# A two-layer decoder trunk: other PSUM tiles for the attention outputs, one copy that joins all turned halves, an earlier 4-byte copy, and 2 MB loads six blocks later

## The chip, the cores and the metric

The kernel runs on one core of one Trainium2 chip. The metric is the device time of one execution in microseconds. The kernel before takes 1239.11 us, the median of three runs (1236.39 to 1240.38).

The engines are named as the profile names them: PE is TensorE's matmul and PEld its weight load, DVE is VectorE, ACT is ScalarE, POOL is GpSimd, SP is SyncE, which here only issues DMAs.

## The reference, cut to what matters

A residual stream x of 256 tokens and 2048 channels, all float32, goes through two layers. Each ends with `x <- LayerNorm(alpha * x + mixer(x))`.

- Layer 1 is a Mamba-2 mixer: an input projection of 2048 to 10304 columns, a causal convolution of four taps, one chunk of 256 tokens with 64 heads of width 64 and state 128, a gate, a grouped norm, and an output projection of 4096 to 2048.
- Layer 2 is sparse attention. A projection gives the query latent (512), the key-value latent (256), an index key, index weights and a gate of 4096 columns. An indexer scores all keys for each query and keeps the 64 best. 32 heads of width 128 attend to the kept keys, each output is gated, and an output projection of 4096 to 2048 follows.

Per head h of layer 2, with P the probabilities over the kept keys:

```
logits = (q_h . k_h) / sqrt(128), masked to the kept keys
P      = softmax(logits)
o_h    = P v_h
out    = concat_h(o_h * silu(gate_h)) @ w_out
```

## The kernel before, in words

**Weights come as a stream.** All weight matrices are cut into 404 units of up to 512 KB. A unit is loaded on SP's queue into one of four raw buffers (`load`, L99), and split for TensorE into two parts of less precision each: ScalarE writes the upper part `hi` (`convert`, L121), VectorE the rest `lo` (`finish`, L145). There are four buffers of each, and a raw buffer is filled again, with the unit four further on, as soon as its `lo` is written. TensorE uses a unit in three products (upper by upper, upper by rest, rest by upper): this is one *block* of the program. `Stream.run` makes the order of all engines: for block i it first writes the conversions up to unit i + 3, then TensorE's products of unit i, and then lets every *side work* that is active take one step. A side work is a Python generator; each `yield` is the end of its step. `st.side(i, ...)` starts one behind block i. Each engine runs its instructions in exactly this order; between engines the tile framework puts semaphores where data or a buffer is shared. It also keeps engines that read one PSUM tile in the order in which the program names them.

**The heads of layer 2** are units too: for each pair of heads one unit with the weights for keys and values (`pair_a`) and one for queries (`pair_b`), and between the pairs units of the gate projection (`g`, L337). Two pairs and three gates, ten blocks, make up one period with four heads. `evac_steps` copies the pair's keys, values and queries out of PSUM: for keys and queries an upper part on ScalarE (L1006), the rest by a subtraction on VectorE (L1007), and a plain 4-byte copy of the first 128 columns on ScalarE (L1008). `head_steps` is one head in nine steps: the logits `lg` (L1017 to L1020); mask and maximum on VectorE (L1028); the exponential on ScalarE (L1033); division on VectorE (L1038), GpSimd's copy of the probabilities into separate upper and lower 16-bit halves (L1042), and a DMA transpose of the halves on SP's queue (L1044); an empty step; GpSimd's copy `ptf` that joins the turned halves to 4-byte numbers (L1048); ScalarE's upper part (L1055), ScalarE's `p2`, the last 128 columns (L1056), and VectorE's rest (L1058); an empty step; the output `o` on TensorE (L1062 to L1065). The steps behind that multiply by the gate on VectorE (`og`, L1068) and split the product for the output projection (L1075, L1077).

**PSUM** has eight tiles in four pools: `acc` with three, `y` with two, `m` with two, `s` with one. In the heads `acc` takes keys, values and gates, `s` the queries, and `y` both the logits and the outputs in turn. `m` serves the transposes and the indexer before the heads and a partial sum at the very end.

**Behind the heads** comes the output projection of layer 2, 64 blocks from `n_heads` on (L616 to L618). When the program reaches `n_heads`, heads 28 to 31 are still under way. There GpSimd's queue issues two DMAs of 2 MB each into `fin` (L1346, L1348): the first layer's result, saved in HBM before, and the gain and bias of the last norm, repeated over all partitions. From `n_heads + 7` on, `x1_steps` loads the first norm's gain and bias in pieces (`gb`, L1249) and applies them to `fin` on VectorE (L1255), 20 steps in all. The residual sums of the output projection need this from `n_heads + 28` on.

Of the kernel before, what the change touches and what calls it, by code (L numbers as in the profile page):

```python
# [9 lines left out]
F32 = mybir.dt.float32  # L10
F32R = mybir.dt.float32r
I32 = mybir.dt.int32
U16 = mybir.dt.uint16
AF = mybir.ActivationFunctionType
# [3 lines left out]
P = 128  # L18
T = 256
# [159 lines left out]
def trunk_kernel(ctx: ExitStack, tc: tile.TileContext, x, xt, w1, wdt, dtp, prm, wo1,  # L179
                 wkv, wcq, wix, wg, wab, wo2, lnr, out):  # L180
    nc = tc.nc
# [12 lines left out]
    st = Stream(nc, wraw, whi, wlo)  # L194
# [5 lines left out]
    def y_tile(name):  # L200
        return p_y.tile([P, 512], F32, tag="y", name=name)

    def m_tile(name):
        return p_m.tile([P, 512], F32, tag="m", name=name)
# [780 lines left out]
    def evac_steps(p, names):  # L985
        for nm in names:
            ps = PR[p]["p" + nm]
            if nm == "v":

                hi, lo = (d2.tile([P, T], F32R, tag=f"hv{k}", name=f"hv{p}_{k}", bufs=3)  # L990
                          for k in range(2))
                t = d2.tile([P, T], F32, tag="hv2", name=f"hv{p}_2", bufs=3)
                nc.scalar.activation(hi, ps[:, 0:T], AF.Copy)
                nc.scalar.activation(t, ps[:, T:2 * T], AF.Copy)
                v.tensor_sub(lo, ps[:, 0:T], hi.bitcast(F32))
                PR[p]["v"] = hi, lo, t
                continue


            pp = ps.rearrange("p (k t) -> p k t", k=2)  # L1000
            w = T if nm == "k" else P
            if nm == "q" and p == 0:
                d2.tile([P, 16], F32, tag="gap2", name="gap2", bufs=1)
            hi, lo = (d2.tile([P, 2, w], F32R, tag=f"h{nm}{k}", name=f"h{nm}{p}_{k}") for k in range(2))
            t = d2.tile([P, 2, P], F32, tag=f"h{nm}2", name=f"h{nm}{p}_2")
            nc.scalar.activation(hi, pp[:, :, T - w:T], AF.Copy)  # L1006
            v.tensor_sub(lo, pp[:, :, T - w:T], hi.bitcast(F32))  # L1007
            nc.scalar.activation(t, pp[:, :, 0:P], AF.Copy)  # L1008
            PR[p][nm] = hi, lo, t
        yield  # L1010

    def head_steps(h):
        p, k = divmod(h, 2)
        (qh, ql, q1), (kh, kl, k1) = ([a[:, k, :] for a in PR[p][nm]] for nm in "qk")
        vh, vl, v2 = (a[:, k * P:(k + 1) * P] for a in PR[p]["v"])
        pl = y_tile(f"lg{h}")
        nc.tensor.matmul(pl[:, 128:384], qh, kh, start=True, stop=False)  # L1017
        nc.tensor.matmul(pl[:, 128:384], qh, kl, start=False, stop=False)
        nc.tensor.matmul(pl[:, 128:384], ql, kh, start=False, stop=True)
        nc.tensor.matmul(pl[:, 0:128], q1, k1, start=True, stop=True)  # L1020
        yield
        lg = d2.tile([P, 384], F32, tag="lg", name=f"lgs{h}")
        mx = d2.tile([P, 2], F32, tag="mx", name=f"mx{h}")
        sm = d2.tile([P, 2], F32, tag="sm", name=f"sm{h}")
        rn = d2.tile([P, 2], F32, tag="rn", name=f"rn{h}")
        parts = ((0, 0, 128), (1, 128, 384))
        for j, a, b in parts:
            v.tensor_tensor_reduce(out=lg[:, a:b], in0=pl[:, a:b], in1=mb[:, a:b],  # L1028
                                   scale=-ATT_SCALE, scalar=3.0e38, op0=ALU.add, op1=ALU.min,
                                   accum_out=mx[:, j:j + 1])  # L1030
        yield
        for j, a, b in parts:
            nc.scalar.activation(lg[:, a:b], lg[:, a:b], AF.Exp, scale=-1.0,  # L1033
                                 bias=mx[:, j:j + 1], accum_out=sm[:, j:j + 1])
        yield
        v.reciprocal(rn, sm)
        for j, a, b in parts:
            v.tensor_scalar(lg[:, a:b], lg[:, a:b], rn[:, j:j + 1], 0.5,  # L1038
                            op0=ALU.mult, op1=ALU.mult)
        halves = cmask.bitcast(U16)  # L1040
        turned = d2.tile([P, 768], U16, tag="ptu", name=f"ptu{h}", bufs=1)
        nc.gpsimd.tensor_copy(halves.rearrange("p (a t) -> p a t", a=2),  # L1042
                              lg.bitcast(U16).rearrange("p (t a) -> p a t", a=2))
        nc.sync.dma_start_transpose(turned.rearrange("p (k t) -> p k t", k=6), halves)  # L1044
        yield
        yield
        pt = d2.tile([P, T], F32, tag="ptf", name=f"ptf{h}", bufs=1)
        nc.gpsimd.tensor_copy(pt.bitcast(U16).rearrange("p (t a) -> p a t", a=2),  # L1048
                              turned.rearrange("p (a t) -> p a t", a=2)[:, :, 0:T])
        yield  # L1050
        if h == 0:
            d2.tile([P, 48], F32, tag="gap3", name="gap3", bufs=1)
        ph, pl = (d2.tile([P, T], F32R, tag=f"prT{j}", name=f"prT{h}_{j}") for j in range(2))
        p2 = par[:, P * k:P * (k + 1)]
        nc.scalar.activation(ph, pt[:, 0:T], AF.Copy)  # L1055
        nc.scalar.activation(p2.bitcast(U16).rearrange("p (t a) -> p a t", a=2),  # L1056
                             turned.rearrange("p (a t) -> p a t", a=2)[:, :, T:384], AF.Copy)
        v.tensor_sub(pl, pt[:, 0:T], ph.bitcast(F32))  # L1058
        yield
        yield  # L1060
        po = y_tile(f"o{h}")
        nc.tensor.matmul(po[:, 0:T], vh, ph, start=True, stop=False)  # L1062
        nc.tensor.matmul(po[:, 0:T], vh, pl, start=False, stop=False)
        nc.tensor.matmul(po[:, 0:T], vl, ph, start=False, stop=False)
        nc.tensor.matmul(po[:, P:T], v2, p2, start=False, stop=True)  # L1065
        yield
        og = d2.tile([P, T], F32, tag="og", name=f"og{h}", bufs=1)
        v.tensor_mul(og, po[:, 0:T], GT.pop(h))  # L1068
        if h == 0:
            OG.append(big.tile([P, KT, 2 * T], F32R, tag="A", name="og0"))  # L1070
        if h == 16:
            OG.append(big.tile([P, KT, 2 * T], F32R, tag="C", name="og1"))
        dst = OG[h // 16][:, h % 16, :]
        yield
        nc.scalar.activation(dst[:, 0:T], og, AF.Copy)  # L1075
        yield
        v.tensor_sub(dst[:, T:2 * T], og, dst[:, 0:T].bitcast(F32))  # L1077
        yield
# [3 lines left out]
    for p in range(NH2 // 2):  # L1082
        src = wab[2 * p]
        i = st.add(wab[2 * p], 1024, pair_a(p), KEYS)
        st.side(i, (evac_steps, p, ("k", "v")))
        i = st.add(wab[2 * p + 1], 1024, pair_b(p), STILL)
        st.side(i, (evac_steps, p, ("q",)))
        if p == 0:
            st.extra[i + 1] = 64
        st.side(i + 3, (head_steps, 2 * p))  # L1090
        st.side(i + 5, (head_steps, 2 * p + 1))
        n = (left * (p + 1)) // 16 - (left * p) // 16
        for _ in range(n):
            add_gate(next(gates))
    n_heads = len(st.units)
# [106 lines left out]
    o = [0]  # L1202
# [38 lines left out]
    d2 = L["d2"] = heads.enter_context(tc.tile_pool(name="d2", bufs=2))  # L1241
# [98 lines left out]
        normed2b()  # L1340
    L["tail2"] = last

    st.run(n_heads)
    fin = big.tile([P, 4, D], F32, tag="B", name="fin")
    L["r"], gbf = fin[:, 0:2, :], fin[:, 2:4, :]
    nc.gpsimd.dma_start(fin[:, 0:2, :], x1_d)  # L1346
    st.side(n_heads + 7, (x1_steps,))
    nc.gpsimd.dma_start(gbf, lnr[2:4, :].rearrange("(o h) t -> o h t", o=1).broadcast_to([P, 2, D]))  # L1348
    st.run(n_heads + 40)
    heads.close()  # L1350
# [1 line left out]
    for i in range(len(st.units) - 4, len(st.units)):  # L1352
        st.homes[i] = wmore, 0
    wturn = ctx.enter_context(tc.tile_pool(name="wturn", bufs=1))
    turned = [[cqT[:, n, :], (cqT[:, 3, :], ckvT[:, 0, :], ckvT[:, 1, :])[n]]
              for n in range(3)] + [wturn.tile([P, P], F32R, tag="idr", name="idr")]
# [95 lines left out]
```

## Time and profile before

| What | Before |
|---|---|
| median of 3 runs | 1239.11 us (1236.39 to 1240.38) |
| profiled execution, its own time | 1239.31 us |
| its span, first to last instruction | 1237.6 us |
| busy: matmul, weight load | 1212.9 us, 1127.6 us |
| busy: VectorE, ScalarE, GpSimd | 919.4 us, 675.6 us, 132.3 us |
| mean granted clock | 0.996 |

The stages on the time axis: layer 1's input side up to about 490 us, its output projection up to about 660 us, layer 2's projections and indexer up to about 780 us, the heads up to about 1045 us with their last outputs until 1077 us, and layer 2's output projection beside them from 1042 us to the end. In rows of waits the columns are: who waited, for what, us in total, times, the longest. In rows of the timeline: start, length, engine, line, operation, what is written and read, and in brackets the idle time before it and what ended it. A wait is put down to the instruction nearest the semaphore's last step, so its neighbour on the same engine may be the one that counted.

### The profile page before, as it was taken

To read this page: it belongs to the slowest core of one execution; us is meant where nothing else is said; L and a number is where in the kernel's file an instruction comes from. 1 tells how busy PE (TensorE), PEld (TensorE's weight loads), DVE (VectorE), ACT (ScalarE), POOL (GpSimd) and SP (SyncE) were. 2 spreads that over 40 slices of the span, in tenths; PEclk is the share of its full clock that TensorE was granted. 3 is DMA by queue.
4 is the path that set the end of the run, shared out by engine and by line. 5 is a ranking of instruction groups with operands and counts; after the bars stand their busy time and mean duration, and the time that the engine had idled before them with its cause. 6 is when DMAs were issued, how large, how long until landed. Compare 5 with 4: busy or idle time off the path is not lost.

```text
span 1237.6 us, 22921 instructions
## 1 busy us (share of the span) xinstructions
PE 1212.9 (98%) x8887; PEld 1127.6 (91%) x8887; DVE 919.4 (74%) x1651; ACT 675.6 (55%) x1178; POOL 132.3 (11%) x173
## 2 busy tenths in 40 slices
PE   9999999999999999999999999999999999899998
PEld 8999999999999999888888999999999998788886
DVE  6978788887898789666458768777777777467467
ACT  6555555665665556444347555666666665443341
POOL 0001011111110110100000000122222212200000
PEclk9999999999999999999999999999999999899999
DMA  8766666566656665576556655665666556975662
GB/s 295 221 200 193 192 201 199 170 222 203 190 185 214 190 203 176 191 266 200 188 193 209 213 175 165 187 173 162 175 177 179 165 169 211 290 231 188 202 190 101
DMA packets 91229, 243.07 MB, mean 196 GB/s; under 512 B 33624, under 2 KB 33760, under 8 KB 90736
## 3 DMA queue, kind: packets, MB, share of 16 engines
q1 hardware_dynamic: 86208, 221.59, 56.6%
q0 software_dynamic: 4912, 20.02, 5.3%
q8 instruction: 70, 1.15, 0.4%
q14 instruction: 39, 0.32, 0.1%
HBM read 231.00 MB, written 4.28 MB: 190 GB/s over the span
## 4 chain that ended last, share of the span: by engine, by line
PE 87%; DVE 6%; ACT 4%; DMA 2%; issue 1%; SPq 0%; POOL 0%; DVEq 0%; ACTq 0%; POOLq 0%
PE acc L337 35%; PE g L337 9%; PE o L616 9%; PE o L617 9%; PE o L618 9%; DVE lo L145 2%; PE y L495 2%; ACT hi L121 2%; DMA ptu<-cmask 1%; PE q L979 1%; PE q L981 1%; PE q L980 1%; DVE lgs L1028 1%; DMA scr<-in_xt_dram 1%; ACT lgs L1033 1%
## 5 line engine op out<-in xcount | busy, mean ns | idle before, releaser
L145 DVE TENSOR_TENSOR lo<-raw,hi 128x1024 fp32r<-128x1024 f32 (+1 forms) x400 | 494.4, 1238 | 250.4 <-ACT hi L121 250.1
L121 ACT ACTIVATE hi<-raw 128x1024 fp32r<-128x1024 f32 (+1 forms) x400 | 417.7, 1050 | 199.7 <-PE o L618 153.1
L337 PE MATMUL acc<-xT,hi 128*128 128x256 f32 (+1 forms) x2496 | 301.4, 277 | 0.0
L337 PEld LDWEIGHTS acc<-xT,hi 128*128 128x128 f32 x2496 | 291.3, 188 | 2.5 <-ACT E L448 1.2
L337 PE MATMUL acc<-xT,lo 128*128 128x256 f32 (+1 forms) x1248 | 156.7, 277 | 0.0
L337 PEld LDWEIGHTS acc<-xT,lo 128*128 128x128 f32 x1248 | 148.3, 188 | 0.1
L337 PE MATMUL g<-x1T,hi 128*128 128x256 f32 (+1 forms) x1024 | 125.6, 277 | 0.0
L337 PEld LDWEIGHTS g<-x1T,hi 128*128 128x128 f32 x1024 | 120.9, 189 | 0.2
L616 PE MATMUL o<-hi,yg 128*128 128x512 f32 x256 | 100.3, 392 | 0.0
L616 PE MATMUL o<-hi,og 128*128 128x512 f32 (+1 forms) x256 | 100.1, 391 | 0.0
L618 PE MATMUL o<-hi,yg 128*128 128x512 f32 x256 | 99.7, 389 | 0.0
L617 PE MATMUL o<-lo,yg 128*128 128x512 f32 x256 | 99.6, 389 | 0.0
L618 PE MATMUL o<-hi,og 128*128 128x512 f32 (+1 forms) x256 | 99.5, 389 | 0.0
L617 PE MATMUL o<-lo,og 128*128 128x512 f32 (+1 forms) x256 | 99.5, 389 | 0.0
L337 PE MATMUL g<-x1T,lo 128*128 128x256 f32 x512 | 71.1, 284 | 0.0
L397 DVE SCALAR_TENSOR_TENSOR ca<-acc,par,ca 128x255 f32<-128x255 f32 x138 | 66.1, 479 | 3.3
L337 PEld LDWEIGHTS g<-x1T,lo 128*128 128x128 f32 x512 | 63.7, 190 | 0.2
L404 ACT ACTIVATE xs<-ca 128x256 f32<-128x256 f32 x32 | 13.4, 419 | 82.9 <-DVE ca L397 49.5
L618 PEld LDWEIGHTS o<-hi,og 128*128 128x128 f32 x256 | 48.5, 189 | 10.1
L617 PEld LDWEIGHTS o<-lo,og 128*128 128x128 f32 x256 | 48.5, 189 | 9.8
L616 PEld LDWEIGHTS o<-hi,og 128*128 128x128 f32 x256 | 48.6, 190 | 9.6
L616 PEld LDWEIGHTS o<-hi,yg 128*128 128x128 f32 x256 | 48.1, 188 | 10.2 <-ACT hi L121 0.2
(296 smaller groups left out, 1793.2 us busy)
## 6 DMA issues: line engine op xcount, KB each, us to landing
raw<-in_w_dram SPq DMA_DIRECT2D x160, 512.0 KB, 4.0
raw<-in_wo_dram SPq DMA_DIRECT2D x128, 512.0 KB, 4.1
raw<-in_wg_dram SPq DMA_DIRECT2D x64, 512.0 KB, 3.6
raw<-in_wab_dram SPq DMA_DIRECT2D x32, 512.0 KB, 4.0
abc<-acs_d POOLq DMA_DIRECT2D x32, 256.0 KB, 4.7
raw<-in_wcq_dram SPq DMA_DIRECT2D x8, 512.0 KB, 4.6
raw<-in_wkv_dram SPq DMA_DIRECT2D x8, 336.0 KB, 3.1
scr<-in_xt_dram SPq DMA_DIRECT2D x4, 512.0 KB, 6.8
```

What stands on the lines that cost most here:

```text
L121: self.nc.scalar.activation(h, r, AF.Copy)
L145: eng.tensor_sub(*self.halfway.pop(i))
L337: nc.tensor.matmul(ps[:, 0:n], wt, xs[:, kt, c * T:c * T + n], start=(kt == 0 and not lo and c == 0), stop=last and c == (1 - lo), skip_gr ...
L397: v.scalar_tensor_tensor(acc[:, d:], ps[:, :T - d], w(k), acc[:, d:], op0=ALU.mult, op1=ALU.add)
L404: nc.scalar.activation(dst, acc, AF.Tanh)
L495: nc.tensor.matmul(py[ks, c * T + s * P:(c + 1) * T], xsT[:, s, c, ks], ms[c][k][:, ws], start=(c == 0 and s == 0), stop=(s == 1), skip_gr ...
L616: nc.tensor.matmul(ps, ah, hs, start=(kk == 2 * first), stop=False)
L617: nc.tensor.matmul(ps, ah, ls, start=False, stop=False)
L618: nc.tensor.matmul(ps, al, hs, start=False, stop=(kk == 31))
L979: nc.tensor.matmul(ps, h[:, o:o + P], cqT[:, kt, 0:T], start=(kt == 0), stop=False)
L980: nc.tensor.matmul(ps, h[:, o:o + P], cqT[:, kt, T:2 * T], start=False, stop=False)
L981: nc.tensor.matmul(ps, l[:, o:o + P], cqT[:, kt, 0:T], start=False, stop=(kt == 3))
```

## The change

Four edits. First, in `evac_steps` the 4-byte copy of the first 128 columns stands ahead of VectorE's subtraction instead of behind it. Second, `ptf` holds all 384 columns: GpSimd joins all halves in one copy of 768 16-bit elements instead of 512, and ScalarE's `p2` reads 128 joined numbers instead of 256 halves. Third, `o` takes an `m` tile instead of a `y` tile. Fourth, the two 2 MB loads are written behind block `n_heads + 5` and not ahead of block `n_heads`, and `x1_steps` starts at `n_heads + 13`.

```diff
@@ evac_steps
             nc.scalar.activation(hi, pp[:, :, T - w:T], AF.Copy)
+            nc.scalar.activation(t, pp[:, :, 0:P], AF.Copy)
             v.tensor_sub(lo, pp[:, :, T - w:T], hi.bitcast(F32))
-            nc.scalar.activation(t, pp[:, :, 0:P], AF.Copy)
@@ head_steps
-        pt = d2.tile([P, T], F32, tag="ptf", name=f"ptf{h}", bufs=1)
+        pt = d2.tile([P, 384], F32, tag="ptf", name=f"ptf{h}", bufs=1)
         nc.gpsimd.tensor_copy(pt.bitcast(U16).rearrange("p (t a) -> p a t", a=2),
-                              turned.rearrange("p (a t) -> p a t", a=2)[:, :, 0:T])
+                              turned.rearrange("p (a t) -> p a t", a=2))
...
         nc.scalar.activation(ph, pt[:, 0:T], AF.Copy)
-        nc.scalar.activation(p2.bitcast(U16).rearrange("p (t a) -> p a t", a=2),
-                             turned.rearrange("p (a t) -> p a t", a=2)[:, :, T:384], AF.Copy)
+        nc.scalar.activation(p2, pt[:, T:384], AF.Copy)
...
-        po = y_tile(f"o{h}")
+        po = m_tile(f"o{h}")
@@ behind the heads
-    st.run(n_heads)
+    st.run(n_heads + 6)
     fin = big.tile([P, 4, D], F32, tag="B", name="fin")
     L["r"], gbf = fin[:, 0:2, :], fin[:, 2:4, :]
     nc.gpsimd.dma_start(fin[:, 0:2, :], x1_d)
-    st.side(n_heads + 7, (x1_steps,))
+    st.side(n_heads + 13, (x1_steps,))
```

How the instruction order moves on the engines that the prediction speaks of. Each row is a line of the program, an operation, what it writes and reads, and in brackets the engines or DMA queues whose semaphores it waits for; numbers in names count buffers, and lines behind the edit are one lower in the changed kernel.

TensorE in the heads, the piece of the difference with one head's output `o` and the logits `lg` of a later head:

```order
-L1062 MATMUL o_10000<-prT_0_9897,hv_0_9451 128x256 [waits DVE_49,Activation_49]
-L1063 MATMUL o_10000<-prT_1_9898,hv_0_9451 128x256
-L1064 MATMUL o_10000<-prT_0_9897,hv_1_9452 128x256
-L1065 MATMUL o_10000<-par,hv_2_9453 128x128 [waits Activation_49]
-L1017 MATMUL lg_10012<-hk_0_9711,hq_0_9768 128x256 [waits DVE_49]
+L1061 MATMUL o_10000<-prT_0_9897,hv_0_9451 128x256 [waits PE_49,Activation_49]
+L1062 MATMUL o_10000<-prT_1_9898,hv_0_9451 128x256
+L1063 MATMUL o_10000<-prT_0_9897,hv_1_9452 128x256
+L1064 MATMUL o_10000<-par,hv_2_9453 128x128 [waits Activation_49]
+L1017 MATMUL lg_10012<-hk_0_9711,hq_0_9768 128x256
```

The order is the same; the first products of `o` and of `lg` no longer name VectorE among what they wait for.

ScalarE at a pair's evacuation, the piece with keys `hk`, values `hv` and queries `hq`:

```order
 L1006 ACTIVATE hk_0_9711<-k_9671 128x512 [waits PE_49]
-L1008 ACTIVATE hk_2_9713<-k_9671 128x256 [waits DVE_49]
+L1007 ACTIVATE hk_2_9713<-k_9671 128x256
 L993 ACTIVATE hv_0_9717<-v_9672 128x256 [waits PE_49]
 L994 ACTIVATE hv_2_9719<-v_9672 128x256
 L121 ACTIVATE hi_9723<-raw_9542 128x1024 [waits DMAHW2_49,Activation_49]
 L1006 ACTIVATE hq_0_9768<-q_9729 128x256 [waits PE_49]
-L1008 ACTIVATE hq_2_9770<-q_9729 128x256 [waits DVE_49]
+L1007 ACTIVATE hq_2_9770<-q_9729 128x256
 L121 ACTIVATE hi_9774<-raw_9585 128x1024 [waits DMAHW4_49,Activation_49]
```

Nothing moves on ScalarE; the 4-byte copies lose their wait for VectorE.

GpSimd at the end of the heads, first before (`cmask` is the copy into halves, `ptf` the join, `fin` the 2 MB loads, `gb_hk` the first norm's pieces):

```order
L1346 DMA fin<-x_d 128x4096 [waits DMASW3_49,PE_49]
L1348 DMA fin<-in_lnr_dram 128x4096
L1048 COPY ptf_13175<-ptu_13108 128x2x256 [waits DMAHW0_49,DVE_49]
L1042 COPY cmask<-lgs_13111 128x768 [waits DVE_49,Pool_49]
L1048 COPY ptf_13239<-ptu_13180 128x2x256 [waits DMAHW3_49,DVE_49]
L1042 COPY cmask<-lgs_13183 128x768 [waits DVE_49,Pool_49]
L1048 COPY ptf_13297<-ptu_13244 128x2x256 [waits DMAHW6_49,DVE_49]
L1249 DMA gb_hk_13349<-in_lnr_dram 128x512 [waits DMASW6_49]
```

and in the changed kernel:

```order
L1048 COPY ptf_13172<-ptu_13108 128x2x384 [waits DMAHW0_49,DVE_49,Activation_49]
L1042 COPY cmask<-lgs_13111 128x768 [waits DVE_49,Pool_49]
L1048 COPY ptf_13236<-ptu_13177 128x2x384 [waits DMAHW3_49,DVE_49,Activation_49]
L1042 COPY cmask<-lgs_13180 128x768 [waits DVE_49,Pool_49]
L1048 COPY ptf_13294<-ptu_13241 128x2x384 [waits DMAHW6_49,DVE_49,Activation_49]
L1345 DMA fin<-x_d 128x4096 [waits DMASW3_49,PE_49]
L1347 DMA fin<-in_lnr_dram 128x4096
L1248 DMA gb_hk_13470<-in_lnr_dram 128x512 [waits DMASW6_49]
```

The two loads stand behind the last three joins instead of ahead of them, and each join carries 384 columns and also waits for ScalarE, which reads its buffer.

## The prediction

> **What bounds the kernel now.** I read the page first: the span, TensorE's busy share, then the stretches, then who TensorE waits for, then single rows of one such wait. The profiled execution took 1239.31 us with a span of 1237.6, so 1.7 us lie outside the span; the median of the runs shown is 0.2 us lower. I work on the profiled execution and take 0.2 off at the end.
>
> ```profile
> span 1237.6 us, 22921 instructions
> PE 1212.9 (98%) x8887; PEld 1127.6 (91%) x8887; DVE 919.4 (74%) x1651; ACT 675.6 (55%) x1178; POOL 132.3 (11%) x173
> 50.00:661.00 611.00, 611.00 (x4637) 571.00 (x4636) 472.23 (x775) 336.92 (x531) 57.38 (x77) 1.00 0.62 202
> 820.00:1031.00 211.00, 198.17 (x1681) 195.39 (x1682) 158.25 (x357) 133.30 (x318) 46.24 (x48) 0.99 0.61 173
> 961.33:964.74 3.41, 3.41 (x19) 3.41 (x18) 1.56 (x2) 3.41 (x10) 0.00 (x0) 0.50 0.33 95
> 1060.32:1067.14 6.82, 5.35 (x14) 4.29 (x15) 3.71 (x7) 5.14 (x12) 3.32 (x4) 0.50 0.80 244
> ...
> PE o L1062 <- DVE og L1068: 10.7, 7, 1.9
> PE o L1062 <- ACT prT L1055: 4.2, 1, 4.2
> PE o L1062 <- DVE rn L1036: 1.9, 6, 0.3
> PE lg L1017 <- DVE mx L1028: 1.8, 6, 0.3
> ```
>
> The stretches (columns: from:to, length, busy us and instructions of TensorE's matmul, its weight load, VectorE, ScalarE, GpSimd, then granted clock) say that TensorE never stops from 50 to 661 us, and stands for 12.8 of 211 us while the heads run. The waits (total, times, longest) name all four stops: the output matmul `o` waits seven times for `og` and six times for what stands as `rn`, the logits `lg` six times for `mx`, and one long wait stands at the end of the heads. Nothing else holds TensorE for more than a pipeline gap, so an edit is worth what it takes from these rows and no more. The granted clock is 0.50 in two stretches, each behind a long wait.
>
> **Part 1: the output accumulator from the other pair of PSUM tiles.** Now `lg` and `o` take turns in the two `y` tiles, so `o` of a head gets the tile that the `o` before it, or a logits, still holds, and must wait until VectorE has read it. Here is a head without the wait and the next with it:
>
> ```profile
> 846.56 0.28 PE L968 MATMUL v<-hi,ckvT 128*128 128x256 f32 x1
> 846.68 0.28 PE L1062 MATMUL o<-prT,hv 128*128 128x256 f32 x1
> 846.79 0.28 PE L1063 MATMUL o<-prT,hv 128*128 128x256 f32 x1
> 847.16 0.37 PE L1017 MATMUL lg<-hk,hq 128*128 128x256 f32 x1
> ...
> 852.36 1.07 PE L337 MATMUL g<-x1T,lo 128*128 128x256 f32 x8
> 855.11 0.36 PE L1062 MATMUL o<-prT,hv 128*128 128x256 f32 x1 [1.68 <-DVE og L1068]
> 855.30 0.28 PE L1063 MATMUL o<-prT,hv 128*128 128x256 f32 x1
> 846.33 0.42 DVE L1068 TENSOR_TENSOR og<-o,sC 128x256 f32<-128x256 f32 x1
> 948.96 0.42 DVE L1058 TENSOR_TENSOR prT<-ptf,prT 128x256 fp32r<-128x256 f32 x1
> 951.49 0.28 PE L1062 MATMUL o<-prT,hv 128*128 128x256 f32 x1
> ```
>
> With two tiles of its own, the `o` at 855.11 needs only the read two heads back, over at 846.75, while TensorE was free at 853.43: 6.7 us to spare. The logits then wait for the logits two heads back, as far away. So the three rows of 10.7, 1.9 and 1.8 us go: **14.4 us**. A stop costs more than its row. Eight matmuls fill 1.07 us, so they start 0.113 apart and the last before the wait starts at 853.15; `o` starts 1.96 us later where 0.12 is normal, and the next 0.19 behind it where 0.11 is normal: 1.92 us lost for a row of 1.68, 0.24 more. Taken for all 19 stops: **4.6 us**. The half clock at 961 follows the longest of these waits (1.9); 3.41 us of work at half speed lose **1.7 us**.
>
> What is late next: `o` also needs the probabilities' rest, written by VectorE at L1058. The tightest head I found has it done at 949.38 and TensorE there at 951.49, 2.1 us to spare. That is the smallest margin behind which the gain can go, and the first rival.
>
> **Part 2: one join of all halves, and 4-byte copies.** GpSimd's copy grows from 512 to 768 elements, ScalarE's copy of the second part loses its 2-byte steps, and the transposes no longer wait for ScalarE.
>
> ```profile
> L1042 POOL COPY cmask<-lgs 128x768 uint16<-128x768 uint16 x32 | 32.6, 1018 | 206.9 <-DVE mx L1028 116.4 <-DVE lgs L1038 90.4
> L1048 POOL COPY ptf<-ptu 128x512 uint16<-128x512 uint16 x32 | 29.2, 912 | 125.7 <-DMA ptu<-cmask 110.9 <-DVE hv L995 6.7 <-DVE lo L145 4.4
> 847.53 1.69 POOL L1042 COPY cmask<-lgs 128x768 uint16<-128x768 uint16 x1 [0.49 <-DVE lgs L1038]
> 848.45 1.04 DVE L1058 TENSOR_TENSOR prT<-ptf,prT 128x256 fp32r<-128x256 f32 x1
> L1056 ACT ACTIVATE par<-ptu 128x256 uint16<-128x256 uint16 x32 | 15.6, 486 | 0.0
> ACT hq L1008 <- DVE hq L1007: 44.6, 16, 3.3
> ACT hk L1008 <- DVE hk L1007: 22.9, 16, 2.1
> L1008 ACT ACTIVATE hq<-q 128x256 f32<-128x256 f32 x16 | 6.2, 385 | 44.6 <-DVE hq L1007 44.6
> ```
>
> The copy of 768 elements at L1042 takes 1.02 us on average and the one of 512 takes 0.91; half as much again would be 1.37. So the join costs 0.1 to 0.46 us a head, GpSimd being idle most of the stage (46 of 211 us); I take 0.3. It lies in front of `L1058`, whose margin is 2.1 us or more: nothing on the path. It also meets VectorE: the `L1058` under the 1.69 us copy took 1.04 us, against 0.42 elsewhere, so up to 32 x 0.46 = 14.7 us of VectorE's time go with it, none of it TensorE's while margins last. The Trainium skill ("SBUF — State Buffer", section "SBUF: two separate sides") speaks against this edit: the port pair that the two engines share is an exclusive lock, held for a whole instruction while the loser fully blocks. The two rows agree with it; by that rule the 0.46 us would stand in front of `L1058` a second time, as blocked VectorE, and rival (a) below would cost 7 x 0.46 = 3.2 us more, 1221.8.
>
> The swap in the evacuation turns a wait round. ScalarE stands 67.5 us (44.6 + 22.9) for VectorE's subtraction before it may copy the last part of the same PSUM tile; now it copies at once, and VectorE waits for a copy of 0.385 us instead, 32 x 0.385 = 12.3 us at most. ScalarE's conversions come up to 3.3 us earlier, so `L1058`, behind them on VectorE, does too. On the path I count nothing for part 2, in either direction; its worth is that it keeps the margin of part 1.
>
> **Part 3: the two 2 MB loads six blocks later.**
>
> ```profile
> fin<-x_d POOLq DMA_DIRECT2D x1, 2048.0 KB, 10.3
> fin<-in_lnr_dram POOLq DMA_DIRECT2D x1, 2048.0 KB, 14.8
> raw<-in_wo_dram SPq DMA_DIRECT2D x2, 512.0 KB, 14.8
> ptu<-cmask SPq DMA_TRANSPOSE x1, 15.3
> ...
> DMA to landing us min/median/max: 2.5/2.6/15.3
> raw<-in_wo_dram SPq DMA_DIRECT2D x3, 512.0 KB, 7.3
> rx<-in_x_dram POOLq DMA_DIRECT2D x2, 1024.0 KB, 11.2
> ACT hi L121 <- PE o L618: 76.5, 48, 2.3
> ```
>
> The first four rows are the DMA issues between 1044 and 1049 us: issued beside the two loads, the transpose took 15.3 us where the median over the heads (next row) is 2.6, and head 29's `o` waited 4.2 us for its probabilities. In the changed order both loads stand behind the last join, so every transpose is done: the wait goes, **4.2 + 0.24 = 4.4 us**, and with it the half clock from 1060.32, in which TensorE worked 5.35 us: **2.7 us**.
>
> The loads now run beside weight loads alone. A weight load is issued when its buffer is free, four blocks ahead; a block of 24 times 0.113 us lasts 2.72, so ScalarE wants it 4 x 2.72 less 2.3 (the two halves of a conversion) = 8.6 us after issue. Conversions in turn wait for TensorE's buffers (last row above), so they are done three blocks ahead, 8.2 less 2.3 = 5.9 us before TensorE. A weight load may thus take 14.5 us before TensorE stands. Beside the two 1 MB loads at 537 us it took 7.3 (TensorE full, first fence); beside these, behind a slow transpose, 14.8. Between 0 and 0.3 us, then, or up to 3 if several loads in a row are late; no transpose stands in their way now, so I take 0. VectorE's work on what is loaded moves with it and lies under the output projection, where VectorE's queue has that 5.9 us of room.
>
> **The sum.** 14.4 + 4.6 + 1.7 + 4.4 + 2.7 = 27.8 us. 1239.3 - 27.8 = 1211.5 for the profiled execution, **1211.3** against the median. A check by another way:
>
> ```profile
> 781.91 0.28 PE L1017 MATMUL lg<-hk,hq 128*128 128x256 f32 x1
> 812.74 0.37 PE L1017 MATMUL lg<-hk,hq 128*128 128x256 f32 x1
> 820.01 0.36 PE L1062 MATMUL o<-prT,hv 128*128 128x256 f32 x1 [1.00 <-DVE og L1068]
> 1030.88 0.36 PE L1062 MATMUL o<-prT,hv 128*128 128x256 f32 x1 [1.67 <-DVE og L1068]
> ```
>
> The first two rows bound the first ten blocks with four logits, when no stop had come: 30.83 us, plus two outputs that were not yet due (846.68 to 847.16 each, 0.48): 31.8. The last two bound six such periods: 35.15 each. That gives 6 x 3.36 = 20.1 us for this stretch where the rows above give 18.3. I keep the lower and put the difference into the range.
>
> **The rivals.** (a) The rest of the probabilities takes over: TensorE comes up to 2.9 us a period earlier, VectorE does not, and the margin of 2.1 turns into a wait of 0.8 + 0.24 us in each of seven periods: 7.3 us back, **1218.6**. For it: GpSimd's longer copy and VectorE's new wait lie right there. Against it: ScalarE, which is in front, loses 67 us of waiting. (b) Weight loads come late behind the moved loads: 3 + 0.24 us and another half-clock stretch of 1.7: **1216.2**. (c) The half clock at 961 is not the wait's doing: of seven waits of 1.0 to 1.9 us only one has it behind it. Then 1.7 us stay, **1213.0**. The Trainium skill ("TensorE: Matmul & The Clock Gate", "What's actually happening") speaks for it: idle means a window of about 3.4 us, longer than that wait. (d) The change does not do what it says, since the reads that `o` waits for are late for the new tiles too; only part 3 is left, 7.1 us: **1232.0**. The 6.7 us speak against it. (e) Slower: VectorE becomes the bound in the heads. It works 158.25 us in 24 heads, 6.6 each, and TensorE without waits needs 31.8 / 4 = 7.95; the new wait and the join add at most 0.39 + 0.46, so 7.45. It decides from 8.8 a head (35.15 / 4) on; at 9.0 it would give 32 x 0.2 = 6.4 us more, **1245.5**. (f) A wait that no row shows fills the gaps: **1239**.
>
> **How the numbers follow.** Forecast 0.67, (a) 0.12, (b) 0.10, (c) 0.05, (d), (e) and (f) 0.02 each. The forecast's own range is 1208 to 1215; with (a) to (c) the range is 1206.5 to 1220. Within 0.3% (3.7 us) of 1239.1 is about what a measurement of this kernel cannot tell from no change: only (f) lies there. Faster 0.96, same 0.02, slower 0.02.
>
> **What would show it.** Right: no row of TensorE waiting for `og`, `rn` or `mx`; six periods of about 31.8 us; ScalarE no longer waiting at the evacuation of `hk` and `hq`, VectorE there instead; every transpose landed in about 2.6 us; granted clock 1.00 between 800 and the end. Wrong: `o` waiting for `prT`, a weight load behind the moved 2 MB with TensorE standing, or a half-clock stretch without a wait before it.

## The result, and the profile after

The changed kernel takes 1211.07 us, the median of four runs (1209.96 to 1211.45). The kernel before, beside it on the same chip, takes 1239.38 us (1236.39 to 1240.38). The ratio is 0.9774 with an interval of [0.9756, 0.9792]. The forecast was 1211.3 us. The profiled execution takes 1210.82 us, 2.0 of them outside the span.

The head of the page, changed kernel:

```profile
span 1208.8 us, 22955 instructions
PE 1202.2 (99%) x8887; PEld 1121.7 (93%) x8887; DVE 923.5 (76%) x1651; ACT 669.5 (55%) x1178; POOL 137.6 (11%) x173
```

TensorE's waits over the whole span (total, times, longest):

```profile
PE zeros L705 <- DVE scr L700: 1.3, 1, 1.3
PE acc_two L347 <- ACT hi L108: 1.0, 2, 0.6
```

Both rows belong to the first 16 us. Behind them TensorE waits for nothing to the end. The stretches, first before and then changed (columns as in the prediction: from:to, length, busy us of TensorE, its weight load, VectorE, ScalarE, GpSimd, then granted clock, DMA share, GB/s):

```profile
820.00:1004.00 184.00, 172.90 (x1463) 170.28 (x1463) 137.10 (x313) 117.16 (x280) 38.05 (x41) 0.99 0.60 172
```

```profile
820.00:1004.00 184.00, 184.00 (x1609) 184.00 (x1608) 153.77 (x341) 122.70 (x303) 48.23 (x47) 1.00 0.70 191
1060.00:1067.00 7.00, 7.00 (x33) 5.79 (x32) 4.19 (x5) 4.15 (x4) 0.00 (x0) 1.00 0.80 297
50.00:661.00 611.00, 611.00 (x4635) 570.88 (x4634) 472.59 (x775) 336.90 (x532) 56.93 (x77) 1.00 0.62 202
```

TensorE stood 11.1 us of these 184 and now stands for none; layer 1 is as it was; between the start and TensorE's last product no stretch has half clock. The two outputs that bound six periods, in the timeline of TensorE, changed kernel:

```profile
818.26 0.28 PE L1061 MATMUL o<-prT,hv 128*128 128x256 f32 x1
1010.70 0.28 PE L1061 MATMUL o<-prT,hv 128*128 128x256 f32 x1
```

They stand 192.44 us apart, 32.07 a period; the same two stood 210.87 apart before. The heads gave 18.4 us in these six periods.

The waits at the evacuation (changed kernel):

```profile
ACT hq L1006 <- PE q L981: 23.0, 16, 2.0
DVE hk L1008 <- ACT hk L1007: 3.1, 6, 0.6
DVE hq L1008 <- ACT hq L1007: 0.6, 1, 0.6
```

ScalarE's 67.5 us of waiting for VectorE are gone. It now waits for TensorE, and VectorE waits 3.7 us for ScalarE.

The moved loads (at the end of a row: KB each, us from issue to landing) and, for the line that issues the transposes, the time to landing:

```profile
fin<-x_d POOLq DMA_DIRECT2D x1, 2048.0 KB, 9.2
fin<-in_lnr_dram POOLq DMA_DIRECT2D x1, 2048.0 KB, 15.6
```

```profile
DMA to landing us min/median/max: 2.5/2.7/5.5
```

ScalarE's wait for weights between 1030 and 1100 us, and from the timelines of VectorE and TensorE one weight unit behind the loads:

```profile
ACT hi L121 <- DMA raw<-in_wo_dram: 7.9, 3, 3.6
```

```profile
1058.44 1.22 DVE L145 TENSOR_TENSOR lo<-raw,hi 128x1024 fp32r<-128x1024 f32 x1 [3.79 <-ACT hi L121]
1062.66 0.39 PE L617 MATMUL o<-lo,og 128*128 128x512 f32 x1
```

No transpose takes longer than 5.5 us (15.3 before; the median is 2.7, where the prediction has about 2.6 for every one). ScalarE did wait for weights beside the moved loads, 7.9 us. The unit at 1058.44 is the tightest: its rest is written at 1059.66, and TensorE reads it at 1062.66, 3.0 us later and without a stop.

### The profile page after: what moved, and what is told of

Read it like the earlier page. It is cut to its first block, busy times and chain, and to the rows that moved or that the text cites. A ratio compares the mean times of both kernels' runs of the same rounds, so it can differ in the third digit from the quotient of the medians.

```text
span 1208.8 us, 22955 instructions
## 1 busy us (share of the span) xinstructions
PE 1202.2 (99%) x8887; PEld 1121.7 (93%) x8887; DVE 923.5 (76%) x1651; ACT 669.5 (55%) x1178; POOL 137.6 (11%) x173
## 4 chain that ended last, share of the span: by engine, by line
PE 98%; DMA 1%; DVE 0%; issue 0%; SPq 0%; ACT 0%; DVEq 0%
PE acc L337 35%; PE g L337 15%; PE o L616 10%; PE o L617 10%; PE o L618 10%; PE y L495 2%; PE q L979 1%; PE q L980 1%; PE q L981 1%; DMA scr<-in_xt_dram 1%; PE v L966 1%; PE k L959 1%; PE v L968 1%; PE k L957 1%; PE k L958 1%; PE v L967 1%
## 5 line engine op out<-in xcount | busy, mean ns | idle before, releaser
L404 ACT ACTIVATE xs<-ca 128x256 f32<-128x256 f32 x32 | 13.4, 419 | 82.9 <-DVE ca L397 49.4
L616 PEld LDWEIGHTS o<-hi,yg 128*128 128x128 f32 x256 | 48.1, 188 | 10.2 <-issue 0.2
L618 PEld LDWEIGHTS o<-hi,yg 128*128 128x128 f32 x256 | 48.1, 188 | 10.1
L618 PEld LDWEIGHTS o<-hi,og 128*128 128x128 f32 x256 | 48.0, 188 | 9.9
L617 PEld LDWEIGHTS o<-lo,yg 128*128 128x128 f32 x256 | 48.1, 188 | 9.7
```

The lines of the kernel that those rows point to most:

```text
L404: nc.scalar.activation(dst, acc, AF.Tanh)
L616: nc.tensor.matmul(ps, ah, hs, start=(kk == 2 * first), stop=False)
L617: nc.tensor.matmul(ps, ah, ls, start=False, stop=False)
L618: nc.tensor.matmul(ps, al, hs, start=False, stop=(kk == 31))
```

## The experiments

The time was as forecast; the question is whether it went for the reasons given. These runs switch the four edits in and out, in us, each the median of its executions (the kernel before, run beside them, took between 1238.5 and 1239.4):

| m tiles | 4-byte copy sooner | join | loads later | time |
|---|---|---|---|---|
| | | | | 1239.4 |
| x | | | | 1237.7 |
| | | | x | 1232.5 |
| | x | x | | 1216.9 |
| x | | | x | 1228.3 |
| x | | x | x | 1228.1 |
| x | x | | x | 1211.0 |
| | x | x | x | 1211.0 |
| | x | | x | 1211.5 |
| x | x | x | x | 1211.1 |

### Part 1 alone: the m tiles

```diff
-        po = y_tile(f"o{h}")
+        po = m_tile(f"o{h}")
```

> Part 1 alone (the outputs in the m tiles, nothing else). My theory: TensorE's rows for og, rn and mx go with their restarts and the half clock behind them, 14.4 + 4.6 + 1.7 = 20.7 us of 1239.4, so 1218.7; the long stop at the heads' end and the half clock behind it stay. Rival (a), the rest of the probabilities takes over because ScalarE has not been relieved: o waits for prT about 1 us in each of seven periods, 1226. Rival (d), the reads are late for the other tiles too: 1239.

Measured: 1237.7 us, ratio 0.9987 [0.9978, 0.9996], so 1.6 us [0.5, 2.7] and not 20.7. TensorE's waits from 700 us on:

```profile
PE g L337 <- DVE gate L804: 9.9, 10, 1.8
PE o L1062 <- ACT prT L1055: 5.4, 1, 5.4
PE g L337 <- DVE sC L804: 1.0, 1, 1.0
PE v L966 <- DVE gate L804: 0.6, 2, 0.3
PE o L616 <- DVE gate L804: 0.3, 1, 0.3
```

and the stretch of the heads, columns as above:

```profile
820.00:1004.00 184.00, 174.25 (x1492) 172.10 (x1491) 137.27 (x309) 118.40 (x283) 37.98 (x41) 1.00 0.60 173
```

The rows for `og`, `rn` and `mx` are gone, as forecast, and the time is not. TensorE now waits for `acc` tiles that hold a gate, which VectorE has not read yet (L804, written to `gate` or `sC`): 11.8 us in place of 14.4. A new wait took the old one's place, on the same engine, VectorE. All theories fell here; rival (a) had the right form with the wrong buffer (`prT`), rival (d) the right size with the wrong reason.

### Part 3 alone: the loads

```diff
-    st.run(n_heads)
+    st.run(n_heads + 6)
...
-    st.side(n_heads + 7, (x1_steps,))
+    st.side(n_heads + 13, (x1_steps,))
```

> Part 3 alone (the two 2 MB loads and x1_steps six blocks later). My theory: the wait of 4.2 us at the heads' end, its restart of 0.24 and 2.7 us of half clock go, 1239.4 - 7.1 = 1232.3, and every transpose lands in under 6 us. Rival: the weight loads take the delay over and TensorE stands for one, about 5 us back, 1237. The og, rn and mx rows stay at about 14 us; if the half clock near 961 us belongs to the long og wait it is there again, if it is not the wait's doing it may be absent or elsewhere.

Measured: 1232.5 us, ratio 0.995 [0.9934, 0.9967], 6.9 us less where 7.1 were forecast. The stop at the end of the heads and the half clock there are gone, the slowest transpose lands in 4.6 us, and behind the start no wait of TensorE for weights is in the trace. The three rows of `og`, `rn` and `mx` stay with 15.1 us, without a half clock behind any of them.

### Part 2 alone, and parts 1 and 3 without it

> Part 2 alone (the join of all halves and the earlier 4-byte copies). My theory as predicted: nothing on the path, 1239.4 within 1 us. Rival: the relief of ScalarE brings VectorE's work forward, og, rn and mx with it, so that part of the 14.4 us of stops goes: at half of them with their restarts 1230. Rival: the longer join slows VectorE beside it, 7 x 0.46 = 3.2 us more, 1242.6.

> Parts 1 and 3 without part 2. If part 2 is what keeps the margin of part 1, as I predicted, o now waits for prT in up to seven periods, up to 7.3 us above the changed kernel: 1213 to 1218.5. Rival: the margin holds without part 2, TensorE waits for nothing and the time is that of the changed kernel, 1211.1 within 0.7 us.

Measured: 1216.9 us for part 2 alone, ratio 0.982 [0.9806, 0.9835]; 1228.3 us without it, ratio 0.9914 [0.99, 0.9929]. Part 2, which the prediction counted at nothing, brings 22.5 us by itself, twice as much as parts 1 and 3 together (11.1). In the run with part 2 alone, TensorE's only wait from 700 us on, at the end of the heads:

```profile
PE o L1061 <- ACT prT L1055: 2.9, 1, 2.9
```

and the stretch of the heads:

```profile
820.00:1004.00 184.00, 184.00 (x1608) 184.00 (x1608) 154.70 (x340) 122.68 (x303) 50.04 (x47) 1.00 0.66 190
```

The outputs still take turns with the logits in the two `y` tiles, and TensorE does not stop once. In the run without part 2 the waits for the gate tile are back (9.5 us in ten stops, 1.9 for `sC`, and three of 0.3).

### Which half of part 2, and are the m tiles needed at all

```diff
 # the 4-byte copy put back (rest as changed)
-            nc.scalar.activation(t, pp[:, :, 0:P], AF.Copy)
             v.tensor_sub(lo, pp[:, :, T - w:T], hi.bitcast(F32))
+            nc.scalar.activation(t, pp[:, :, 0:P], AF.Copy)
 # the join put back to 512 elements, p2 from halves (another run)
-        pt = d2.tile([P, 384], F32, tag="ptf", name=f"ptf{h}", bufs=1)
+        pt = d2.tile([P, T], F32, tag="ptf", name=f"ptf{h}", bufs=1)
...
 # the outputs back in the y tiles (another run)
-        po = m_tile(f"o{h}")
+        po = y_tile(f"o{h}")
```

> The changed kernel with the 4-byte copies put back behind VectorE's subtraction; the join, the m tiles and the moved loads stay. New theory: VectorE and ScalarE, waiting for each other in turn, are what sets the pace of the heads; ScalarE's 67 us of waiting for the subtraction come back, its weight conversions come late, VectorE waits for them, and TensorE waits for a gate tile that VectorE has not released: as in the run without part 2, 1228, VectorE's waits for hi near 33 us between 820 and 1004. Rival: it is the join (fewer ScalarE steps, a turned buffer that comes free sooner) that brought the time, then 1211 to 1213.

> The changed kernel without the join: GpSimd joins 512 elements, ScalarE writes the last 128 columns from halves; the earlier 4-byte copies, the m tiles and the moved loads stay. New theory: the join is worth nothing, 1211.1 within 1 us, TensorE waits for nothing in the heads. Rival: the join brought part of the gain, above 1214.

> The changed kernel with the outputs back in the y tiles, taking turns with the logits. New theory: TensorE's waits for og, rn and mx came from VectorE running late, not from the tiles; with VectorE on time the tiles do not matter: 1211.1 within 1 us. My prediction, read as it stands: without part 1 the 14.4 us of waits and their restarts stay, about 1230. Between them: the y tiles are free just in time and some outputs wait 0.3 us, 1212 to 1214.

> The kernel before with two edits only: the earlier 4-byte copies and the moved loads; outputs in the y tiles, join of 512 elements. New theory: these two are the whole change, 1211.0 within 1 us, and TensorE waits for nothing from 780 us on. Rival: the join or the m tiles are needed by one another's absence (each was left out alone at no cost), then some outputs wait for og again, 1213 or more.

Measured: without the earlier 4-byte copy 1228.1 us, ratio 0.992 [0.9905, 0.9935]; without the join 1211.0, ratio 0.9784 [0.9767, 0.98]; without the m tiles 1211.0, ratio 0.9784 [0.977, 0.9799]; with nothing but the earlier copy and the moved loads 1211.5, ratio 0.9779 [0.9764, 0.9794]. Two lines exchanged in `evac_steps` and the moved loads are the whole gain. The exchange is worth 21.0 us (1232.5 to 1211.5), the join nothing, the m tiles nothing once the exchange is there.

How a wait of ScalarE holds TensorE is seen in both engines' rows of the kernel before. Timeline of ScalarE, then of VectorE, at one pair's evacuation:

```profile
847.75 0.57 ACT L1006 ACTIVATE hk<-k 128x512 fp32r<-128x512 f32 x1
850.46 0.39 ACT L1008 ACTIVATE hk<-k 128x256 f32<-128x256 f32 x1 [2.13 <-DVE hk L1007]
...
852.22 0.40 ACT L1006 ACTIVATE hq<-q 128x256 fp32r<-128x256 f32 x1
855.89 0.39 ACT L1008 ACTIVATE hq<-q 128x256 f32<-128x256 f32 x1 [3.28 <-DVE hq L1007]
856.17 1.05 ACT L121 ACTIVATE hi<-raw 128x1024 fp32r<-128x1024 f32 x1
```

```profile
851.43 0.42 DVE L995 TENSOR_TENSOR hv<-v,hv 128x256 fp32r<-128x256 f32 x1 [1.00 <-ACT hv L994]
...
855.43 0.42 DVE L1007 TENSOR_TENSOR hq<-q,hq 128x256 fp32r<-128x256 f32 x1
857.25 1.23 DVE L145 TENSOR_TENSOR lo<-raw,hi 128x1024 fp32r<-128x1024 f32 x1 [1.40 <-ACT hi L121]
```

ScalarE has the queries' upper part at 852.6 and then stands until VectorE, which has other work in its queue, reaches the subtraction at 855.43. Behind the standing copy on ScalarE is a weight conversion (856.17), and VectorE, done with its own queue, stands 1.40 us for it. Each engine waits for the other in turn. The waits of both between 820 and 1004 us, before:

```profile
DVE lo L145 <- ACT hi L121: 33.7, 34, 1.4
DVE hv L995 <- ACT hv L994: 10.0, 10, 1.0
DVE hk L1007 <- ACT hk L1006: 0.8, 3, 0.4
...
ACT hq L1008 <- DVE hq L1007: 32.9, 11, 3.3
ACT hk L1008 <- DVE hk L1007: 13.8, 10, 2.1
ACT gate L802 <- PE g L337: 9.6, 5, 2.6
...
ACT sC L802 <- PE g L337: 2.0, 1, 2.0
...
```

and in the changed kernel:

```profile
DVE lo L145 <- ACT hi L121: 25.2, 44, 1.2
...
ACT gate L802 <- PE g L337: 35.2, 14, 3.2
ACT hq L1006 <- PE q L981: 14.9, 11, 2.0
ACT sC L802 <- PE g L337: 10.0, 4, 3.1
...
```

Before, VectorE's 137.1 us of work and 44.5 of waiting for ScalarE fill 181.6 of the 184 us, while ScalarE stands 46.7 us for VectorE's subtractions and 11.6 for TensorE. In the run with part 1 alone ScalarE waits for TensorE not once in these 184 us (49.4 us for the subtractions), and TensorE still stands for 9.75. So the two engines hold each other up in a loop that needs no TensorE, and a period of four heads at its pace takes longer than TensorE's own work: 35.15 us in the kernel before against 32.07 in the changed one. `og`, `mx` and the gate are read late because VectorE is late; which PSUM tile TensorE then stands for is only a matter of which is read last. After the exchange ScalarE stands 60.1 us for TensorE and not at all for the subtractions: TensorE sets the pace. That VectorE's work and waits fill the stretch is no sign by itself, for they still do (153.8 and 28.3 us); what changed is for whom ScalarE stands.

### Standing, or PSUM tiles released late?

The order of the two reads also changes when the tiles of keys and queries come free. Here the copy stands behind the subtraction again, but one block later, when it has nothing to wait for:

```diff
-            nc.scalar.activation(t, pp[:, :, 0:P], AF.Copy)
             v.tensor_sub(lo, pp[:, :, T - w:T], hi.bitcast(F32))
             PR[p][nm] = hi, lo, t
+            later = t, pp
         yield
+        nc.scalar.activation(later[0], later[1][:, :, 0:P], AF.Copy)
+        yield
```

(In the step with keys and values only the keys have such a copy.)

> The changed kernel with the 4-byte copies of keys and queries put one block later, behind the subtraction but not waiting for it, since it is long done by then; the PSUM tiles of keys and queries are released a block (2.7 us) later. If ScalarE's standing is what cost the time: no waits of ScalarE for the subtraction, about 1211 to 1213. If it is the time at which the PSUM tiles are released: TensorE waits for the keys' tile, which the gate or the next unit wants, and 1220 or more.

Measured: 1211.7 us, ratio 0.9788 [0.9774, 0.9803]. The last pair's copy of the keys starts 2.6 us behind their upper part here and 2.7 in the kernel before, that of the queries 3.0 and 3.7, so the tiles come free nearly as late as they did. Later release costs nothing; it was the standing.

### How much standing, and how much work, the loop bears

```diff
-            nc.scalar.activation(t, pp[:, :, 0:P], AF.Copy)
+            if nm == "q":      # "k" in the other run
+                nc.scalar.activation(t, pp[:, :, 0:P], AF.Copy)
             v.tensor_sub(lo, pp[:, :, T - w:T], hi.bitcast(F32))
+            if nm != "q":      # "k" in the other run
+                nc.scalar.activation(t, pp[:, :, 0:P], AF.Copy)
```

> The changed kernel with the earlier 4-byte copy for the queries alone; the keys' copy stands behind the subtraction. Theory of a pace that is set by ScalarE and VectorE waiting for each other: before, ScalarE stood 44.6 us for the queries and 22.9 for the keys; if each microsecond of standing costs the same share of the 17 us between this kernel without the swap (1228.1) and with it (1211.1), the queries are worth 11 us and the remaining stand of the keys costs 6: 1217. Rival: the loop has slack, and with the longer stand gone TensorE sets the pace again: 1211 to 1212.

> The changed kernel with the earlier 4-byte copy for the keys alone; the queries' copy stands behind the subtraction. By the same share the stand for the queries costs 11 us: 1222. Rival: the loop has slack for one of the two: 1211 to 1214.

Measured: queries alone 1211.5 us, ratio 0.9777 [0.9763, 0.9792]; keys alone 1212.0, ratio 0.9782 [0.9766, 0.9798]. So the cost is not a share of the standing: with either copy moved the loop is short enough, and TensorE sets the pace. In the run with the keys alone it is short enough by little. ScalarE's waits between 820 and 1004 us, then the stretch:

```profile
ACT hq L1011 <- DVE hq L1009: 31.3, 11, 3.7
ACT og L1077 <- DVE og L1070: 8.5, 10, 1.3
ACT hq L1006 <- PE q L981: 6.6, 8, 1.2
ACT gate L802 <- PE g L337: 5.6, 4, 1.8
...
```

```profile
820.00:1004.00 184.00, 183.70 (x1602) 183.50 (x1602) 152.88 (x336) 123.92 (x305) 51.98 (x46) 1.00 0.66 186
```

ScalarE still stands 31.3 us for the queries (32.9 before), and TensorE loses 0.30 us in these 184. A long row of waits thus does no harm by itself; with the 13.8 us for the keys beside it, the loop was longer than TensorE's work. How long a period of the loop is in this run no row shows: the two engines' rows look much like a loop here too, and only TensorE's 0.30 us say that it sets the pace.

```diff
-            v.tensor_sub(pl, pt[:, 0:T], ph.bitcast(F32))
+            for _ in range(2):
+                v.tensor_sub(pl, pt[:, 0:T], ph.bitcast(F32))
...
+        for _ in range(2):
             v.tensor_mul(og, po[:, 0:T], gt)
```

> The changed kernel with two of VectorE's operations in each head done twice over (the rest of the probabilities and the product with the gate), 0.66 to 0.84 us more of VectorE a head, 6.7 to about 7.4 us where TensorE needs 8.0. By busy time alone (the reading of my rival e) VectorE still has room: 1211 to 1213. If VectorE's waits for ScalarE's conversions (28 us of 184, 1.2 a head) count as used time too, 7.4 + 1.2 = 8.6 us a head and VectorE sets the pace: 24 heads or more by 0.6, 1225 or above. Between: part of those waits shrinks as VectorE runs later.

Measured: 1211.7 us, ratio 0.978 [0.9765, 0.9795]. The heads, and VectorE's waits there:

```profile
820.00:1004.00 184.00, 184.00 (x1608) 184.00 (x1607) 171.63 (x388) 123.94 (x305) 49.13 (x47) 1.00 0.68 190
```

```profile
DVE lo L145 <- ACT hi L121: 7.8, 17, 0.8
```

VectorE at 171.63 of 184 us, 93%, does not hold TensorE: the added work comes out of its waits (25.2 down to 7.8 us), which are slack as long as ScalarE itself only waits for TensorE. Before, at 75%, VectorE held TensorE. Its busy share tells neither.

## Why the prediction was right, and where its reasons were not

**The sum** was right to 0.2 us because it was taken from TensorE's own stops: whoever removes them all gains that much. Its attribution was wrong in two steps that balance, and that they balance is luck: part 2, at nothing in the sum, was in the bundle, and parts 1 and 3, to which the sum gives everything, bring 11.1 us of the 27.8 without it. The signs of being right came, a median transpose of 2.7 us and a period of 32.07 for 31.8 among them, but they name what TensorE does and not which edit does it: the run with the exchange and the moved loads alone shows no wait of TensorE either.

**Part 1, "So the three rows of 10.7, 1.9 and 1.8 us go".** The rows go by the m tiles (part 1 alone), the time does not: 1.6 us by themselves, 4.2 beside the moved loads (1232.5 to 1228.3), nothing once ScalarE no longer stands. The step that failed is the one behind it, "What is late next". It looked at one successor, the probabilities' rest with 2.1 us to spare, and took the smallest margin found there for the smallest there is; the gate tiles had less. The engine that all those rows name was late as a whole, and a tile more for one reader does not make it sooner.

**Part 2, "On the path I count nothing for part 2".** This is the other failed step: the exchange brings 21.0 us. The row for it was quoted, 67.5 us of ScalarE's standing, and the text even says that conversions come 3.3 us earlier. What was not asked is whether VectorE waits for these conversions, which would have closed the loop. That "its worth is that it keeps the margin of part 1" is right in the letter, for without it the m tiles bring 4.2 us, but part 1 has no worth to be kept.

**The join** was priced rightly at nothing. GpSimd's rows:

```profile
L1048 POOL COPY ptf<-ptu 128x768 uint16<-128x768 uint16 x32 | 41.2, 1286 | 105.1 <-DMA ptu<-cmask 77.6 <-DVE lo L145 11.1 <-DVE lgs L1038 8.2
```

1.286 us against 0.912 before, 0.37 a head where 0.1 to 0.46 was allowed. VectorE's bill is 2.8 us in 184 us of the heads (153.77 busy against the 150.94 of the next row), far under the 14.7 allowed for all of them. The heads in the run without the join:

```profile
820.00:1004.00 184.00, 184.00 (x1608) 184.00 (x1607) 150.94 (x340) 125.75 (x303) 43.69 (x47) 1.00 0.66 190
```

**The restart cost.** Six periods gave 18.4 us; the rows with 0.24 us for each of their 16 stops and the 1.7 us of half clock made 18.3, the cross-check by unstalled periods 20.1. The rows were the better measure: a period takes 32.07 us and not 31.8.

**The 1.7 us of half clock at 961.** They are gone in the changed kernel, and they were gone too in the traced execution of the run with the loads alone, where all the waits were still there. So they need a wait, but do not follow every such wait (last section). Rival (c) is wrong in that nothing of them stays in the changed kernel, and right in that the wait's length alone does not bring them.

**Part 3** was right in size and in mechanism: 6.9 us for 7.1, no slow transpose, and weight loads that come late for ScalarE but not for TensorE (3.0 of 5.9 us of margin left). Rival (b) needs 3 us more delay than was there.

**The other rivals.** (a) did not come: no `o` waits for `prT` in the changed kernel. (e), VectorE as the bound from 8.8 us of work a head on, was weighed by busy time; VectorE was already the bound before, together with ScalarE, at the 6.6 us a head that the prediction gives, and is not at 7.5 in the last run (171.63 in 23 heads).

## What to carry to other kernels

Rows of waits on the engine that sets the end give the size of a gain and not its cause: before an edit is credited, follow the engine that releases late one step back and ask what it waits for itself. Two engines with long rows of waits for each other in the same stretch, while the engine that should set the pace stands, are to be suspected of a loop, and its bound is not seen in any busy share; look for the instruction in one queue that stands for the other with work behind it. Such a loop costs only what it is longer than the next bound, so half of a fix may bring all of the gain, and a row of 31 us of waits may cost next to nothing in one kernel and be part of a loop that costs 21 us in another.

## What the runs showed of the hardware

The half-clock stretches begin on a grid: 961.33 and 1060.32 in the kernel before are 98.99 us apart, 29 times 3.413, and while TensorE has work they last 3.41 or 6.82. Laid over that grid, TensorE's stops sort by how much of one grid window they fill. Two windows, first of the kernel before, then of the run with the loads alone:

```profile
957.92:961.33 3.41, 1.52 (x14) 1.35 (x13) 2.93 (x8) 0.42 (x3) 0.26 (x1) 1.00 0.55 172
```

```profile
920.97:924.38 3.41, 1.75 (x15) 1.58 (x15) 2.80 (x6) 0.74 (x2) 1.80 (x1) 1.00 0.65 178
```

The first, idle for 1.89 of 3.41 us (55%), is followed by half clock; the second, idle for 1.66 (49%), is not. In the traces of the kernel before and of the five runs with parts 1, 2, 3 alone, with parts 1 and 3, and with the 4-byte copy put back, I took every window between 8 and 1200 us in which TensorE was idle for more than 1.2 us: four windows at full clock were idle for 0.55 or more of their length, and half clock followed each; 19 were idle for 0.36 to 0.49, and it followed none. The border is not sharp by this busy time. In the run with part 2 alone, when the last products are done, half clock does not follow a window idle for 1.92 us (56%):

```profile
1209.86:1213.27 3.41, 1.49 (x4) 0.38 (x2) 2.06 (x3) 0.00 (x0) 0.00 (x0) 1.00 0.65 254
1213.27:1216.68 3.41, 0.00 (x0) 0.00 (x0) 0.00 (x0) 0.00 (x0) 0.00 (x0) 1.00 0.14 54
```

So a stop a little longer than half a window seems to halve the clock or not by where it falls, which fits the run with the loads alone: its longest stop, 1.81 us, lies across a border of its grid, 0.67 us on one side and 1.14 on the other. It fits too that executions of one kernel differ: of 27 of the kernel before, run beside the experiments, six show a mean granted clock of 0.999 (1236.0 to 1238.1 us) and the others 0.994 to 0.997 (1237.8 to 1240.8). No run tested this by itself. The Trainium skill ("TensorE: Matmul & The Clock Gate", "What's actually happening") states a free-running window of 3413 ns, with which the grid agrees; its table "Why this matters for your kernels" asks for no idle gaps over about 3 us, and here 1.89 us were enough.
